# Layer 0 of a two-layer hybrid backbone: two S5 products summed by matmuls in PSUM, and the first norm's squares summed by matmuls

## The chip, the core and the metric

The kernel runs on one core of one Trainium2 chip. Its metric is the device time of one launch in microseconds; shorter is better. The engines are named as the profile names them: PE is TensorE's matmul, PEld its weight load, DVE is VectorE, ACT is ScalarE, POOL is GpSimd, SP the engine that issues the DMAs. L333 is line 333 of the kernel.

## The reference, cut to what matters

Two layers over 640 tokens (128 of a prompt and 512 of a sample) with 1024 channels. Every sub-layer starts with an RMS norm over the channels, scaled and shifted by a modulation that comes from a condition vector. Layer 0 projects the normed tokens into an S5 head group (`u`, 512 channels) and an attention head group (`q`, `k`, `v`). What matters here is the norm and how the S5 input matrix is made:

```python
def _rmsnorm(x, g):
    x32 = x.astype(jnp.float32)
    y = x32 * lax.rsqrt(jnp.mean(x32 * x32, axis=-1, keepdims=True) + EPS)
    return (y * g.astype(jnp.float32)).astype(x.dtype)
...
    lam_bar = jnp.exp(lam * jnp.exp(log_dt.astype(f32))[:, None])
    b_bar = ((lam_bar - 1) / lam)[..., None] * lax.complex(b_re.astype(f32), b_im.astype(f32))
    bu = jnp.einsum('gnp,blgp->blgn', b_bar, u.astype(jnp.complex64))
...
        hp = _modulate(_rmsnorm(xp, norm_mix_g[l]), mp[0], mp[1])
```

The kernel takes eight tokens at a time in the S5 part, so it multiplies `b_bar` by powers 0 to 8 of `lam_bar`. Real part of such a complex product: two real products and their sum.

## The kernel before, in words

Tokens lie along the free dimension and channels on the partitions, so `x` is eight tiles of 128 x 640, each worked on in two halves of 320. A long product is three matmuls of 320 columns (L205 to L207), since both factors are split into a high part (`whi`, `h00h`) and a low rest (`wlo`, `h00l`). Weights come by `weight`: a DMA into `raw`, a copy on ACT into `whi` (L194), a subtraction on POOL (or DVE) into `wlo` (L196).

The order of the instructions on each engine is not written out by hand. A scheduler sets it from priorities and from its own timeline; each engine then works its list off strictly in that order, so an instruction that waits holds up all behind it.

**The start (`start`).** ACT squares the 16 halves of `x`. The first square of each half of the tokens goes into `acc`, and each later one into `sq` and is added to `acc` by DVE (`sumsq_add`, L325). `rstd_bcast` then sums `acc` over the partitions: three matmuls for each half of the tokens, with `acc` as the stationary operand and two columns of ones as the moving one (L333), so that tokens come out on partitions. DVE makes mean plus EPS of it (L335) and an inverse square root in twelve small steps (L176 to L182), PE transposes the result into a bank (L339) and ACT copies it to `bc` (L385). The modulation runs beside this: for two blocks of columns and two halves of the channels at a time, `mod_half` multiplies the condition with weights (L282), ACT copies the row (L290), PE transposes it (L292), DVE reduces and adds it (L295, L296, L395). Then come the normalising steps, for each channel block and half (`norm_step`: L349 on DVE, L351 and L355 on ACT, L353 on DVE for even blocks, L357 on POOL for odd ones), and as each pair of blocks is done, its long products of the first three projections.

**The S5 part.** `s5_params` makes `lam_bar`, the scaled B (L716 to L722) and the powers (L744 to L749) out of some 130 small operations on DVE, at the same priority as the start. Then, for four channel blocks and two directions, `s5_unit` makes the input matrix `bp` as two products (L786, L787) and their sum (L788) on DVE, has PE transpose it in eight pieces (L793) into two banks of the tag `pb`, and has ACT copy them to `bpt` (L794), the weight of L810. L799 to L801 make the output matrix in the same manner. The units are spread over the projection of q, k, v and the attention behind it.

PSUM has eight banks: two of each of the tags `pg`, `pa`, `pb` and `pc`.

Of the kernel before, what the change touches and what calls it, by code (L numbers as in the profile page):

```python
# [11 lines left out]
F32 = mybir.dt.float32  # L12
F32R = mybir.dt.float32r
I32 = mybir.dt.int32
AF = mybir.ActivationFunctionType
ALU = mybir.AluOpType
# [5 lines left out]
HB = 320  # L22
EPS = 1e-6
NEG = -1e30
MAGIC = 12582912.0
HALVES = (slice(0, 320), slice(320, 640))
# [122 lines left out]
class Build:  # L149
# [177 lines left out]
    def rstd_bcast(self, st, tag="pc"):  # L327

        nc = self.nc
        ps = self.ps(tag)  # L330
        tiles = (0, 128, 192)
        for i, t0 in enumerate(tiles):
            nc.tensor.matmul(ps[:, 2 * i:2 * i + 2], st[0][:, t0:t0 + 128], self.ones2, start=True, stop=True)  # L333
        a = self.sp.tile([128, 3], F32, name="nrm_a", tag="nrm_a", bufs=2)
        nc.vector.tensor_scalar(a, ps[:, 0:6:2], 1.0 / 1024, EPS, op0=ALU.mult, op1=ALU.add)  # L335
        y = self.rsqrt(self.sp, a, 3, "nrm")
        bc = self.ps(tag)
        for i in (2, 1, 0):
            nc.tensor.transpose(bc[:, tiles[i]:tiles[i] + 128], y[:, i:i + 1].to_broadcast([128, 128]), self.ident)  # L339
        return bc  # L340
# [26 lines left out]
    def start(self, x, dst, P):  # L367

        nc = self.nc
        st = [self.sumsq(h) for h in range(2)]  # L370
        for k in range(8):
            for h in range(2):
                self.sumsq_add(st[h], x[k][:, HALVES[h]], nc.vector, P)
        self.mraw = "mraw", 16
        self.WX, self.WT = P, ("mraw", "mraw", 16)
        ws = [self.weight(self.A["wine"][j], 8, j) for j in range(2)]
        pairs = [[(0, 4 * n + i, kh) for n in range(2) for kh in range(2)] for i in range(4)]
        for pair in pairs:
            for m in pair:
                self.mod_load(*m, P)  # L380
        bcs = []
        for h in range(2):
            p = self.rstd_bcast(st[h], ("pg", "pa")[h])
            bc = P.tile([128, HB], F32, name="bc", bufs=2)
            nc.scalar.activation(bc, p[:, :HB], AF.Copy)  # L385
            bcs.append(bc)
        banks = [[self.ps(t) for _ in range(2)] for t in ("pg", "pa", "pb")]
        done = [0] * 3
        for i, pair in enumerate(pairs):
            md = [P.tile([128, 2, 2], F32, name=f"md{i}{n}") for n in range(2)]  # L390
            for m in pair:
                self.mod_half(*m, P, row=(P, "mrow", 2), dst=md[m[1] // 4])
            if i == 1:
                ws.append(self.weight(self.A["wine"][2], 8, 2))
            nc.vector.scalar_tensor_tensor(md[1], md[1], 1.0, self.ng[:, 0, 2 * i:2 * i + 2].unsqueeze(2).to_broadcast([128, 2, 2]),  # L395
                                           op0=ALU.add, op1=ALU.mult)
            for k in (2 * i, 2 * i + 1):
                for h in range(2):
                    self.norm_step(h, k, x[k], bcs[h], md[1][:, k % 2], md[0][:, k % 2], dst[k], True)
                for j, w in enumerate(ws):  # L400
                    for kk in range(done[j], k + 1):
                        for h in range(2):
                            self.mm_step(w, dst, h, kk, 8, banks[j][h], HB)
                    done[j] = k + 1
        w = self.weight(self.A["wine"][3], 8, 3)
        self.proj_u()
        for j in range(4):
            for h in range(2):
                if j == 3:
                    p = self.ps("pg")  # L410
                    for k in range(8):
                        self.mm_step(w, dst, h, k, 8, p, HB)
                else:
                    p = banks[j][h]
                self.ev_u(j, h, p[:, :HB])
# [354 lines left out]
    def s5_unit(self, b, d, P, U, tb):  # L770

        nc = self.nc
        V = nc.vector
        G = nc.gpsimd
        M, AD, SU = ALU.mult, ALU.add, ALU.subtract
        p0 = d * 32 + b * 8
        ps = slice(p0, p0 + 8)
        bc4 = lambda a, ax, sh: a.unsqueeze(ax).to_broadcast(sh)

        sh = [128, 8, 8, 16]  # L780
        ks = slice(0, 8) if d == 0 else slice(1, 9)
        bp = self.tl([128, 8, 128], "bp")
        t1 = self.tl([128, 8, 9, 16], "s5tmp")
        bpv = bp.rearrange("p g (s q) -> p g s q", s=8)
        B1 = self.Bb1[:, :1024].rearrange("p (a b) -> p a b", b=16)[:, ps]
        V.tensor_tensor(bpv, bc4(self.pr[:, ps, ks], 3, sh), bc4(B1, 2, sh), op=M)  # L786
        V.tensor_tensor(t1[:, :, :8], bc4(self.pi[:, ps, ks], 3, sh), bc4(self.Bb2[:, ps], 2, sh), op=M)  # L787
        V.tensor_tensor(bpv, bpv, t1[:, :, :8], op=AD)  # L788
        bpt = self.tl([128, 8, 128], "bpt")
        for r in range(2):  # L790
            pp = self.ps("pb")
            for i in range(4):
                nc.tensor.transpose(pp[:, 128 * i:128 * i + 128], bp[:, 4 * r + i], self.ident)  # L793
            nc.scalar.activation(bpt[:, 4 * r:4 * r + 4].rearrange("p a b -> p (a b)"), pp, AF.Copy)  # L794

        sh = [128, 8, 9, 16]
        ct = self.tl([128, 8, 9, 16], "ct")
        t2 = self.tl([128, 8, 9, 16], "s5tmp")
        V.tensor_tensor(ct, bc4(self.pr[:, ps], 3, sh), bc4(self.C1[:, ps], 2, sh), op=M)  # L799
        V.tensor_tensor(t2, bc4(self.pi[:, ps], 3, sh), bc4(self.C2[:, ps], 2, sh), op=M)  # L800
        V.tensor_tensor(ct, ct, t2, op=SU)  # L801

        W = self.tl([128, 8, 82], "s5g")
        e0 = 1 - d
        for r in range(2):
            pw = self.ps("pb")
            for i in range(4):
                g = 4 * r + i
                n = 128 if g < 7 else 82
                nc.tensor.matmul(pw[:, 128 * i:128 * i + n], bpt[:, g], U[:, g * 82:g * 82 + n],  # L810
                                 start=True, stop=True)
            nc.scalar.activation(W[:, 4 * r:4 * r + 4, e0:e0 + 81],
                                 pw.rearrange("p (a b) -> p a b", a=4)[:, :, :81], AF.Copy)
        ex, ez = (0, 65) if d == 0 else (64, 81)
        nc.scalar.activation(W[:, :, ex:ex + 1], self.s5x0[:, ps].unsqueeze(2), AF.Copy)
        V.memset(W[:, :, ez:ez + 1], 0.0)

        def segs(t):
            so = t[:, :, 0:65], t[:, :, 65:82]
            return so  # L820
        def tab(t):
            return (t, t[:, :, 0:17]) if d == 0 else (t[:, :, ::-1], t[:, :, 16::-1])
        sgn = self.cst[:, 400:401]
        def swap(src, name):
            o = self.tl([128, 8, 82], "s5g")
            nc.sync.dma_start(out=o[0:64], in_=src[64:128])
            nc.sync.dma_start(out=o[64:128], in_=src[0:64])
            return o
        def rotate(src, op, out):
            sw = swap(src, "sw")  # L830
            for so, c_, s_, w_ in zip(segs(src), tab(tb[:, 0]), tab(tb[:, 1]), segs(sw)):
                V.tensor_tensor(so, so, c_, op=M)
                V.scalar_tensor_tensor(w_, w_, sgn, s_, op0=M, op1=M)
            V.tensor_tensor(out, src, sw, op=op)
        Z = self.tl([128, 8, 82], "s5g")
        rotate(W, SU, Z)
        d0 = self.tl([128, 8, 82], "s5g")
        nc.scalar.activation(d0, self.s5rho[:, ps].unsqueeze(2).to_broadcast([128, 8, 82]), AF.Copy)
        V.memset(d0[:, :, ex:ex + 1], 0.0)
        V.memset(d0[:, :, ez:ez + 1], 0.0)  # L840
        Y = self.tl([128, 8, 82], "s5g")
        fl = lambda t: t.rearrange("p a b -> p (a b)")
        if d == 0:
            V.tensor_tensor_scan(fl(Y), fl(d0), fl(Z), 0.0, op0=M, op1=AD)
        else:
            V.tensor_tensor_scan(fl(Y)[:, ::-1], fl(d0)[:, ::-1], fl(Z)[:, ::-1], 0.0, op0=M, op1=AD)
        S = self.tl([128, 656], "s5s")
        Sv = S.rearrange("p (a b) -> p a b", a=8)
        rotate(Y, AD, Sv)
        fin = 81 if d == 0 else 65  # L850
        nc.scalar.activation(self.s5fin[:, p0:p0 + 8].unsqueeze(2), Sv[:, :, fin:fin + 1], AF.Copy)
        return ct, S
# [1147 lines left out]
```

## Time and profile before

| | us |
|---|---|
| median of 3 runs | 1971.04 |
| range of the runs | 1970.84 to 1973.8 |
| profiled execution, its own time | 1975.42 |
| span in its trace | 1973.2 |
| PE, PEld busy | 1798.4, 1696.1 |
| DVE, ACT, POOL busy | 1279.3, 875.5, 760.1 |

The span runs from the first to the last instruction of the profiled execution. An engine's busy time counts only its working instructions, not waits or the issue of DMAs. A busy PE is not a PE at its peak, since matmuls overlap and their ends are modelled; its clock is shown apart, as the granted share of 2.4 GHz (1.00, or 0.50 at 1.2 GHz).

### The profile page before, as it was taken

What the parts mean: (1) busy time and instruction counts of PE and PEld (TensorE: products, weight loads), DVE (VectorE), ACT (ScalarE), POOL (GpSimd) and SP (SyncE); (2) the same over time, 40 slices, a digit from 0 to 9 for tenths busy, and PEclk for the clock granted to TensorE, in tenths of its full rate; (3) what the DMA queues carried; (4) which work ended last, traced back from release to release, by engine and by line L of the source; (5) the groups of instructions that cost most, each with busy time, mean ns of one, the idle gap of its engine ahead of it and who ended that gap; (6) DMA issues with size and microseconds to landing.
All of it is one profiled execution on the core that took longest, in us unless ns stands there. A gap on an engine that the chain in (4) does not pass through costs nothing. (4 is left out here: it accounts for less than half of the span.)

```text
span 1973.2 us, 35750 instructions
## 1 busy us (share of the span) xinstructions
PE 1798.4 (91%) x13556; PEld 1696.1 (86%) x13556; DVE 1279.3 (65%) x2797; ACT 875.5 (44%) x1956; POOL 760.1 (39%) x609
## 2 busy tenths in 40 slices
PE   5789799989999999997878888798989899999998
PEld 3789677978999999997877888787878799999997
DVE  8998777269273644547589988674667927364553
ACT  4344466344243443535454455344324425344362
POOL 2522101541343343453455555522245334343451
PEclk9989899999999999998998999999999999999999
DMA  8446886533332222332576468758844122222221
GB/s 319 131 122 167 248 264 205 201 121 126 109 117 76 77 85 82 135 117 72 163 208 197 117 196 239 222 166 269 274 137 149 54 97 76 86 76 86 76 97 54
DMA packets 206983, 286.60 MB, mean 145 GB/s; under 512 B 54878, under 2 KB 138236, under 8 KB 206812
## 3 DMA queue, kind: packets, MB, share of 16 engines
q1 hardware_dynamic: 206812, 284.33, 45.4%
q8 instruction: 107, 1.75, 0.4%
q14 instruction: 64, 0.52, 0.1%
HBM read 228.87 MB, written 46.82 MB: 140 GB/s over the span
## 5 line engine op out<-in xcount | busy, mean ns | idle before, releaser
L196 POOL TENSOR_TENSOR wlo<-raw,whi 128x1024 fp32r<-128x1024 f32 (+1 forms) x153 | 359.3, 2351 | 509.1 <-ACT whi L194 462.3
L194 ACT ACTIVATE whi<-raw 128x1024 fp32r<-128x1024 f32 (+1 forms) x153 | 153.1, 1001 | 329.1 <-PE pg L206 146.8
L207 PE MATMUL pg<-hidh,wlo 128*128 128x320 f32 (+2 forms) x576 | 178.8, 311 | 0.6 <-POOL wlo L196 0.6
L205 PE MATMUL pg<-hidh,whi 128*128 128x320 f32 (+2 forms) x576 | 179.0, 311 | 0.0
L206 PE MATMUL pg<-hidl,whi 128*128 128x320 f32 (+2 forms) x576 | 178.9, 311 | 0.0
L423 DVE SCALAR_TENSOR_TENSOR x<-pg,mod,x 128x128 f32<-128x128 f32 (+2 forms) x132 | 53.7, 436 | 182.2 <-PE pg L207 182.2
L205 PE MATMUL pg<-h10h,whi 128*128 128x320 f32 x472 | 158.4, 336 | 14.7 <-DVE cb L1722 7.0
L207 PE MATMUL pg<-h10h,wlo 128*128 128x320 f32 x472 | 155.4, 329 | 1.7 <-POOL wlo L196 1.7
L206 PE MATMUL pg<-h10l,whi 128*128 128x320 f32 x472 | 155.7, 330 | 0.0
L205 PE MATMUL pa<-hidh,whi 128*128 128x320 f32 x448 | 138.0, 310 | 1.1 <-ACT whi L194 1.1
L207 PE MATMUL pa<-hidh,wlo 128*128 128x320 f32 x448 | 138.4, 309 | 0.0
L206 PE MATMUL pa<-hidl,whi 128*128 128x320 f32 x448 | 138.2, 309 | 0.0
L423 DVE SCALAR_TENSOR_TENSOR x<-pa,mod,x 128x128 f32<-128x128 f32 (+2 forms) x108 | 43.9, 435 | 133.1 <-PE pa L207 133.1
L508 POOL TENSOR_TENSOR wq<-S,wq 128x512 fp32r<-128x512 f32 x52 | 71.3, 1371 | 115.3 <-ACT wq L507 115.3
L205 PEld LDWEIGHTS pg<-h10h,whi 128*128 128x128 f32 x472 | 95.8, 203 | 18.3 <-DVE cb L1722 8.0
L207 PEld LDWEIGHTS pg<-hidh,wlo 128*128 128x128 f32 x576 | 108.2, 188 | 1.6 <-POOL wlo L196 1.1
L205 PEld LDWEIGHTS pg<-hidh,whi 128*128 128x128 f32 x576 | 108.3, 188 | 0.9 <-issue 0.8
L206 PEld LDWEIGHTS pg<-hidl,whi 128*128 128x128 f32 x576 | 108.2, 188 | 0.4 <-DVE hidl L569 0.3
L1322 DVE SCALAR_TENSOR_TENSOR cv<-cb,cw,cv 128x642 f32<-128x642 f32 x90 | 95.8, 1065 | 10.4 <-ACT cv L1319 9.2
L207 PEld LDWEIGHTS pg<-h10h,wlo 128*128 128x128 f32 x472 | 95.4, 202 | 2.1 <-POOL wlo L196 1.9
L206 PEld LDWEIGHTS pg<-h10l,whi 128*128 128x128 f32 x472 | 95.7, 203 | 0.6 <-issue 0.4
L205 PEld LDWEIGHTS pa<-hidh,whi 128*128 128x128 f32 x448 | 83.9, 188 | 2.7 <-ACT whi L194 1.8
(743 smaller groups left out, 5745.4 us busy)
## 6 DMA issues: line engine op xcount, KB each, us to landing
raw<-in_wff SPq DMA_DIRECT2D x104, 512.0 KB
mraw<-in_wmod SPq DMA_DIRECT2D x96, 512.0 KB
raw<-in_wino SPq DMA_DIRECT2D x33, 512.0 KB
rawx<-in_wff SPq DMA_DIRECT2D x24, 512.0 KB
raw<-in_wine SPq DMA_DIRECT2D x16, 512.0 KB
cka<-pd SPq DMA_DIRECT2D x28, 256.0 KB
ckb<-pd SPq DMA_DIRECT2D x28, 256.0 KB
s5g<-s5g SPq DMA_DIRECT2D x32, 164.0 KB
```

The lines of the kernel that those rows point to most:

```text
L194: nc.scalar.activation(hi[:, :kt], raw[:, :kt], AF.Copy)
L196: (nc.vector if self.lov and self.nw % self.lov else nc.gpsimd).tensor_tensor(lo[:, :kt], raw[:, :kt], hi[:, :kt], op=ALU.subtract)
L205: nc.tensor.matmul(p[:, :n], hi[:, k], xh[:, s], start=(k == 0), stop=False)
L206: nc.tensor.matmul(p[:, :n], hi[:, k], xl[:, s], start=False, stop=False)
L207: nc.tensor.matmul(p[:, :n], lo[:, k], xh[:, s], start=False, stop=(k == kt - 1))
L423: nc.vector.scalar_tensor_tensor(x[m][:, s], p[:, ls], g, x[m][:, s], op0=ALU.mult, op1=ALU.add)
L508: (V if j % 2 else nc.gpsimd).tensor_tensor(t[:, 4:8], src, t[:, 0:4], op=SU)
L1322: V.scalar_tensor_tensor(cv, cb[m][:, t:t + 642], cw[:, t:t + 1], cv, op0=M, op1=AD)
```

## The change

Two edits, both in layer 0.

In `start` the squares are no longer added up by DVE. All 16 go into `sq` (four buffers), and for each of them three matmuls add its sums over the partitions to what is in PSUM already: six banks are held for that, one for each half and token tile, with `start` at the first channel block and `stop` at the last. `rstd_bcast` reads three banks instead of one tile, and both halves use the tag `pc` for the transposes.

In `s5_unit` the sum on DVE is gone. Each of the eight pieces is made by two plain matmuls with the identity into the same place of the bank, the first with the first product as stationary operand, the second with the other.

```diff
     def rstd_bcast(self, st, tag="pc"):
...
+        if len(st) == 3:
+            for i, p in enumerate(st):
+                nc.vector.tensor_scalar(a[:, i:i + 1], p[:, 0:1], 1.0 / 1024, EPS, op0=ALU.mult, op1=ALU.add)
+        else:
+            ps = self.ps(tag)
+            for i, t0 in enumerate(tiles):
+                nc.tensor.matmul(ps[:, 2 * i:2 * i + 2], st[0][:, t0:t0 + 128], self.ones2, start=True, stop=True)
+            nc.vector.tensor_scalar(a, ps[:, 0:6:2], 1.0 / 1024, EPS, op0=ALU.mult, op1=ALU.add)
...
     def start(self, x, dst, P):
...
-        st = [self.sumsq(h) for h in range(2)]
+        tiles = (0, 128, 192)
+        sums = [[self.ps(t) for t in ("pg", "pa", "pb")] for h in range(2)]
         for k in range(8):
             for h in range(2):
-                self.sumsq_add(st[h], x[k][:, HALVES[h]], nc.vector, P)
+                sq = P.tile([128, HB], F32, name="sq", tag="sq", bufs=4)
+                nc.scalar.activation(sq, x[k][:, HALVES[h]], AF.Square)
+                for p, t0 in zip(sums[h], tiles):
+                    nc.tensor.matmul(p[:, 0:2], sq[:, t0:t0 + 128], self.ones2, start=(k == 0), stop=(k == 7))
...
-            p = self.rstd_bcast(st[h], ("pg", "pa")[h])
+            p = self.rstd_bcast(sums[h], "pc")
...
     def s5_unit(self, b, d, P, U, tb):
...
-        V.tensor_tensor(bpv, bpv, t1[:, :, :8], op=AD)
...
-                nc.tensor.transpose(pp[:, 128 * i:128 * i + 128], bp[:, 4 * r + i], self.ident)
+                o = pp[:, 128 * i:128 * i + 128]
+                nc.tensor.matmul(o, bp[:, 4 * r + i], self.ident, start=True, stop=False)
+                nc.tensor.matmul(o, t1[:, 4 * r + i, :8].rearrange("p s q -> p (s q)"), self.ident, start=False, stop=True)
```

The scheduler makes another order of it. DVE, where the norm's sums are read, before:

```order
L640 SCALAR_TENSOR_TENSOR s5t_803<-s5t_799,s5t_801 128x64
L633 TENSOR_SCALAR s5t_805<-s5t_803 128x64
L335 TENSOR_SCALAR nrm_a<-pg 128x3
L640 SCALAR_TENSOR_TENSOR s5t_807<-s5t_805,s5t_803 128x64
L176 TENSOR_SCALAR nrm_t<-nrm_a 128x3
```

and after (`s5t` are the small tiles of `s5_params`; L636 and L642 of the changed kernel are L627 and L633 of the one before, L334 reads a sum):

```order
L636 TENSOR_TENSOR s5t_949<-s5t_929,s5prm 128x64
L636 TENSOR_TENSOR s5t_951<-s5t_939,s5prm 128x64
L636 TENSOR_TENSOR s5t_953<-s5t_949,s5t_951 128x64
L334 TENSOR_SCALAR nrm_a<-pg 128x1
L636 TENSOR_TENSOR s5t_955<-s5t_953,s5t_937 128x64
L642 TENSOR_SCALAR s5t_957<-s5t_955,cst 128x64
L334 TENSOR_SCALAR nrm_a<-pa 128x1
```

Ahead of the first of these reads stood 24 operations of `s5_params`; now 84 stand there, up to its division and the scale of B.

DVE at the last pair of channel blocks of the norm, before (L349 normalises, `pw` and `pwr` are the powers):

```order
L353 SCALAR_TENSOR_TENSOR h00l_125<-nf,md_569,h00h_124 128x192
L353 SCALAR_TENSOR_TENSOR h00l_125<-nf,md_569,h00h_124 128x320
L349 SCALAR_TENSOR_TENSOR nf<-x_103,md_570,bc 128x320
L719 TENSOR_TENSOR Bb_924<-s5bc_753,s5t_911 128x1024
L744 TENSOR_TENSOR pw<-pwr 128x32
L745 TENSOR_TENSOR pw<-pwi 128x32
L746 TENSOR_TENSOR pwr<-pw 128x32
```

and after (L353 of the changed kernel is L349 of the one before, L730 and L731 are L721 and L722, L753 to L758 are L744 to L749):

```order
L295 TENSOR_REDUCE mtmp<-pc 128x4
L730 TENSOR_TENSOR Bb_960<-Bb_960,Btmp 128x1024
L755 TENSOR_TENSOR pwr<-pw 128x32
L296 TENSOR_TENSOR md_606<-mtmp,bmod 128x4
L731 TENSOR_SCALAR Bb_960<-Bb_960,cst 128x1024
L756 TENSOR_TENSOR pw<-pwr,pwi 128x32
L757 TENSOR_TENSOR pw<-pwi,pwr 128x32
L404 SCALAR_TENSOR_TENSOR md_606<-md_606,ng 128x4
L758 TENSOR_TENSOR pwi<-pw 128x32
L353 SCALAR_TENSOR_TENSOR nf<-x_102,md_606,bc 128x128
```

The scaled B and the powers of the first direction, which all stood behind the norm's last step, now stand ahead of the last pair of blocks.

PE at the first S5 unit, before (`h00h` and `h00l` are the normed tokens, 311 long products stand ahead of L793):

```order
L207 MATMUL pg<-h00h_124,wlo 128x320
L205 MATMUL pg<-h00h_126,whi 128x320
L206 MATMUL pg<-h00l_127,whi 128x320
L793 MATMUL pb<-cst,bp 128x128 x8
L207 MATMUL pg<-h00h_126,wlo 128x320
```

and after, with 221 long products ahead of it:

```order
L206 MATMUL pg<-h00l_115,whi 128x320
L802 MATMUL pb<-cst,bp 128x128 x2
L207 MATMUL pg<-h00h_114,wlo 128x320
L205 MATMUL pg<-h00h_116,whi 128x320
L206 MATMUL pg<-h00l_117,whi 128x320
L207 MATMUL pg<-h00h_116,wlo 128x320
L205 MATMUL pg<-h00h_118,whi 128x320
L803 MATMUL pb<-cst,s5tmp 128x128
L802 MATMUL pb<-cst,bp 128x128
L803 MATMUL pb<-cst,s5tmp 128x128
```

The eight transposes have become two kinds of matmul, L802 and L803, that alternate, and the unit stands 90 long products earlier in PE's list.

ACT at the squares, after (L194 copies weights; before, all 16 squares stood ahead of both copies):

```order
L379 ACTIVATE sq<-x_99 128x320 x2
L379 ACTIVATE sq<-x_100 128x320
L194 ACTIVATE whi<-raw 128x1024
L379 ACTIVATE sq<-x_100 128x320
L194 ACTIVATE whi<-raw 128x1024
L379 ACTIVATE sq<-x_101 128x320 x2
L379 ACTIVATE sq<-x_102 128x320 x2
L379 ACTIVATE sq<-x_103 128x320 x2
```

Six of the squares now stand behind the second copy.

## Rows read from the trace of the kernel before

**Rows 1.** The page: busy us, share, instructions; busy tenths in 40 slices.

```profile
PE 1798.4 (91%) x13556; PEld 1696.1 (86%) x13556; DVE 1279.3 (65%) x2797; ACT 875.5 (44%) x1956; POOL 760.1 (39%) x609
...
DVE  8998777269273644547589988674667927364553
```

**Rows 2.** Windows, us: length, busy PE, PEld, DVE, ACT, POOL, clock, DMA, GB/s.

```profile
31.00:64.60 33.60, 29.36 (x223) 22.05 (x216) 33.36 (x103) 18.08 (x44) 17.66 (x16) 1.00 0.46 174
81.50:201.20 119.70, 107.58 (x790) 105.16 (x788) 108.16 (x156) 45.69 (x91) 34.15 (x19) 0.94 0.54 149
201.20:260.00 58.80, 46.55 (x389) 37.31 (x388) 47.14 (x95) 29.64 (x84) 3.55 (x4) 0.91 0.86 257
99.70:104.00 4.30, 4.28 (x19) 4.28 (x20) 4.30 (x9) 1.79 (x4) 0.00 (x0) 0.55 0.01 2
135.00:140.00 5.00, 4.86 (x21) 4.86 (x22) 5.00 (x14) 1.98 (x6) 0.00 (x0) 0.50 0.30 88
```

**Rows 3.** Timeline of the start: start us, us, engine line op, [idle before <-releaser].

```profile
6.45 0.83 ACT L320 ACTIVATE acc<-x 128x320 f32<-128x320 f32 x2 [2.54 <-DMA x<-in_xT]
6.55 0.48 DVE L640 SCALAR_TENSOR_TENSOR s5t<-s5t,s5t 128x64 f32<-128x64 f32 x2
...
12.88 0.35 DVE L627 TENSOR_TENSOR s5t<-s5prm,s5t 128x64 f32<-128x64 f32 x2
13.15 0.89 DVE L325 TENSOR_TENSOR acc<-acc,sq 128x320 f32<-128x320 f32 x2
...
15.70 4.68 POOL L196 TENSOR_TENSOR wlo<-raw,whi 128x1024 fp32r<-128x1024 f32 x2 [14.44 <-ACT whi L194]
15.81 1.06 ACT L194 ACTIVATE whi<-raw 128x1024 fp32r<-128x1024 f32 x1 [0.19 <-DMA raw<-in_wine]
15.82 4.64 DVE L640 SCALAR_TENSOR_TENSOR s5t<-s5t,s5t 128x64 f32<-128x64 f32 x2
...
16.40 1.42 PE L333 MATMUL pa<-cst,acc 128*128 128x2 f32 x6
...
17.75 1.93 PE L282 MATMUL pc<-mraw,scond 128*32 128x256 f32 x16
...
20.61 0.15 DVE L335 TENSOR_SCALAR nrm_a<-pg 128x3 f32<-128x3 f32 x1
...
24.02 0.90 PE L339 MATMUL pg<-cst,nrm_y 128*128 128x128 f32 x3 [4.34 <-DVE nrm_y L182]
...
30.25 1.73 DVE L349 SCALAR_TENSOR_TENSOR nf<-x,md,bc 128x128 f32<-128x128 f32 x5
...
57.15 0.54 DVE L349 SCALAR_TENSOR_TENSOR nf<-x,md,bc 128x320 f32<-128x320 f32 x1
...
64.59 0.41 ACT L1055 ACTIVATE us<-pg 128x128 f32<-128x128 f32 x1 [5.21 <-PE pg L207]
...
86.21 1.23 DVE L786 TENSOR_TENSOR bp<-pwr,Bb 128x1024 f32<-128x1024 f32 x1
```

**Rows 4.** Timeline of PE at a later norm, full clock.

```profile
403.08 0.72 PE L333 MATMUL pc<-cst,acc 128*128 128x2 f32 x6
403.66 0.39 PE L206 MATMUL pa<-ct,whi 128*128 128x320 f32 x1
```

**Rows 5.** Line 788: duration in ns (min, median, max), first and last start.

```profile
L788 DVE TENSOR_TENSOR bp<-bp,s5tmp x8: 1214/1218/1227, 98.5 to 238.5; 128x1024 f32<-128x1024 f32 x8
```

**Rows 6.** Timeline of PE at the S5 units.

```profile
99.72 1.97 PE L793 MATMUL pb<-cst,bp 128*128 128x128 f32 x8 [5.42 <-DVE bp L788]
105.50 1.91 PE L810 MATMUL pb<-s5s,bpt 128*128 128x128 f32 x16
...
135.14 1.11 PE L793 MATMUL pb<-cst,bp 128*128 128x128 f32 x4 [4.35 <-DVE kk L910]
...
241.85 1.04 PE L793 MATMUL pb<-cst,bp 128*128 128x128 f32 x8
```

**Rows 7.** Waits of PE, 60 to 260 us: total, times, longest.

```profile
PE pc L1105 <- ACT qs L1090: 6.2, 2, 5.1
```

More of the change, by code (lines that the diff above doesn't have):

```diff
@@ L329, in rstd_bcast @@
         nc = self.nc
-        ps = self.ps(tag)
         tiles = (0, 128, 192)
-        for i, t0 in enumerate(tiles):
-            nc.tensor.matmul(ps[:, 2 * i:2 * i + 2], st[0][:, t0:t0 + 128], self.ones2, start=True, stop=True)
         a = self.sp.tile([128, 3], F32, name="nrm_a", tag="nrm_a", bufs=2)
-        nc.vector.tensor_scalar(a, ps[:, 0:6:2], 1.0 / 1024, EPS, op0=ALU.mult, op1=ALU.add)
+        if len(st) == 3:
[6 more added lines that the diff above has]
+            nc.vector.tensor_scalar(a, ps[:, 0:6:2], 1.0 / 1024, EPS, op0=ALU.mult, op1=ALU.add)
         y = self.rsqrt(self.sp, a, 3, "nrm")
@@ L386, in start @@
             bcs.append(bc)
+        del sums, p
         banks = [[self.ps(t) for _ in range(2)] for t in ("pg", "pa", "pb")]
```

## The prediction

> **What bounds the kernel now.** I read the page first: its busy times and its slices, for the engine that is busy nearly everywhere. TensorE (PE) is at 91% of the span, VectorE (DVE) at 65%, but the first three slices of DVE (some 150 us) read 8, 9, 9 [rows 1]. So the kernel is PE's, except at its head, where both edits lie. Next I cut that head into stretches, by where PE's long products stand. From 31.0 to 64.6 us DVE is busy 33.4 of 33.6 us and PE 29.4; from 81.5 (240 long products done, of the layer's 768) to 201.2 (all 768 done) PE is busy 107.6 of 119.7 at a granted clock of 0.94; from 201.2 to 260.0, the attention, 46.6 of 58.8 at 0.91 [rows 2]. So PE stands still for 12.1 us in the middle stretch and 12.2 us in the last. Its clock takes 119.7 x 0.06 = 7.2 us and 58.8 x 0.09 = 5.3 us more. After 260 us PE is nearly full, and what its queue has lost by then it keeps: I count every microsecond at the head as one at the end. Last I looked at what ends PE's idle time. The two long waits of the middle stretch, 5.42 and 4.35 us, stand right before the S5 transposes of line 793, and DVE ended both [rows 6].
>
> **The S5 matrices.** DVE loses the addition of line 788, eight times, 1.22 us each, 9.8 us [rows 5]. PE pays. Eight transposes ran in 1.04 us at full clock, so one costs (1.04 - 0.27) / 7 = 0.11 us, the 0.27 being the tail of the last. A plain f32 product of the same size is two records: line 810 had 16 of them in 1.91 us, (1.91 - 0.27) / 15 = 0.109 each, 0.22 for a product [rows 6]. A unit had 8 transposes (0.9 us) and gets 16 products (3.5 us), 2.6 us more; eight units, **+21.0 us** of PE time at full clock. At half the clock a transpose took (1.97 - 0.42) / 7 = 0.22 us [rows 6], so a unit would cost 5.2 us more there; I take the full clock, as only two of the eight groups started slow.
>
> What hides these 21 us is idle time of PE behind DVE. If DVE is early enough at line 793, the two waits go (9.8 us), and so does most of the slow clock behind them: 4.3 us at 0.55 from 99.7 and 5.0 us at 0.50 from 135 [rows 2] are 1.9 + 2.5 = 4.4 us. Of the 17.5 us that the attention loses, the longest wait, 5.1 us on ACT behind the last projection [rows 7], can be filled, since products of the sixth and seventh unit now stand there; I take 4 us. So **R = 18 us** come back. At the least one DVE wait goes with its clock, 9 us; at the most all of 19.3 and some 14 of 17.5, 33 us.
>
> **The norm's squares.** DVE loses 14 additions at a pace of 0.45 us, 6.2 us; PE gains 96 records in place of 12. ACT squares as before, 0.42 us each from 6.45 on. At the clock that PE shows there, six records take 1.35 us (16.40 to 17.75) [rows 3]: 96 x 0.225 = 21.6 us, from 6.9 to 28.5 us. At full clock six took 0.58 (403.08 to 403.66) [rows 4]: 9.3 us in all, and then ACT's order decides, where six squares now stand behind the second weight copy (15.81 + 1.06): 16.9 + 6 x 0.42 + 0.6 = 20 us. Which clock it is, no row shows; both ends are kept.
>
> It matters less than it seems, because DVE's order moved too. The first sum is read behind 84 S5 operations, where it stood behind 24. An S5 operation takes 0.18 to 0.24 us (pairs of 0.35 and 0.48), so 60 more are 10.5 to 14.1 us, less the 6.2 of the additions: the read at 20.61 goes to 24.9 to 28.5 [rows 3]; I take 27 us, **6.4 later**. Behind it 51 operations stand before both inverse roots are there; 33 took 3.4 us between the read and the transposes at 24.02, 0.10 each, so these take 5.4 us: 32.4. From the transposes to the first normalising step it was 6.2 us. The modulation products that ran ahead of the sums (16 in 1.93) now lie in that way, and the lag of the second root is gone from it; I take 6 us. So the first normalising step comes at 38 us instead of 30.25, **+8**, with 6 and 10 as ends.
>
> From there to the last normalising step it was 26.9 us [rows 3], DVE full [rows 2]. Of what lies between, 46 small S5 operations are gone (8 to 11 us), but 27 small ones on the powers and four large ones on the scaled B (lines 719 to 749) stand ahead of the last pair's steps: 27 x 0.18 to 0.24 and four of line 788's size, 4.9 us [rows 5], make 10 to 11 us. That is +1. And POOL's long operations come into this stretch: two S5 operations, 0.48 us as a pair at 6.55, took 4.64 us at 15.82 beside two of POOL that took 4.68 [rows 3], so each POOL operation cost DVE 2.1 us; three more of them are 6.3. PE, which waited for weights at the end of the stretch, now has them early; for that I take 3 us back. Together +4, with -5 and +11 as ends. So the third projection ends at about 77 us instead of 64.6: **D = +12 us**, from 1 to 21. On DVE itself the lighter load shows behind that: its line 786, at 86.2 before [rows 3], should come at about 80, and with PE 12 us late that is why PE's waits should go.
>
> **Sum.** D + 21.0 - R = 12 + 21 - 18 = **+15 us**; the ends are 1 + 21 - 33 = -11 and 21 + 21 - 9 = +33. The profiled run took 1975.4 us (span 1973.2), 4.4 above the median of 1971.0; on it the sum makes 1990.4, on the median **1986.0**.
>
> **Rivals.** (a) *DVE was what PE followed all along.* If the norm's chain is not late (D = 1, its additions gone) and DVE, 16 us lighter, lets PE run through all the waits (R = 31), the time is 1971 + 1 + 21 - 31 = 1962, faster. For it: DVE at 33.4 of 33.6 us. Against: PE itself is busy for 107.6 of 119.7, and its order lets the last normalising steps come behind 60 S5 operations. It wins where R passes 21 us plus D. (b) *The head is not late, but PE then meets DVE again*: D = 2, R = 17, 1977. In PE's order only 221 long products stand ahead of the first S5 group, 311 before, so an early PE waits there. (c) *Nothing comes back*: PE comes to the S5 groups just as early as its operands, and the waits only change their place: D = 12, R = 4, 2000.
>
> What the last one would do at its worst, the whole price of 21 us on top of D with no idle time filled, is 2004. The Trainium skill says the same without a condition (Perfetto Trace Analysis, section Transposes: a logical transpose should be a transpose and not a standard matmul). The two waits of 5.42 and 4.35 us speak against taking it unconditionally, since in them a product costs nothing.
>
> **How the numbers follow.** My forecast, +15, has 0.60; (a) 0.16; (b) 0.15; (c) 0.09. What this kernel's measurement can tell from no change is about 0.2%, 4 us. The forecast's own spread (D and R) lies nearly all above +4; (b) is above it at its middle and within it for a third; (a) is faster for nearly all of it. With some of the forecast's lower end, that makes faster 0.17, the same 0.08, slower 0.75. The range runs from 1967, which takes in (b) and the nearer part of (a), to 2002, which takes in (c); some 0.18 is left outside, mostly (a).
>
> **What would show it.** In the changed profile: (1) the first normalising step at about 38 us and the last at 65 to 77; if the last is at 57 as before, D is wrong. (2) A group of 16 products in about 3.5 us, two records each. (3) No wait of PE on DVE at the S5 groups; if waits of 3 us or more stand there, (b) or (c). (4) The records of the sums at 1.35 us for six up to 28 us, or 0.58 and done at 20. (5) All 768 long products done at 210 to 220 us instead of 201. The order of PE changes far beyond layer 0's head, and what that shifts later I count as nothing; several microseconds of either sign there would make the sum wrong without any of these steps.

## The result, and the profile after

The changed kernel took 1994.6 us (median of 4 runs, 1992.56 to 1998.26), the kernel before, on the same chip, 1972.42: 22 us more, ratio 1.0104 with a 95% interval of 1.0081 to 1.0127. Measured again on another occasion it took 1995.66 against 1974.32, ratio 1.0116 (1.0093 to 1.0138). The profiled execution took 1993.4 us, its span is 1991.6. The forecast was 1986.0, +15 us, in a range of 1967 to 2002.

The page after, answering to [rows 1] (busy us, share, instructions; busy tenths in 40 slices):

```profile
PE 1835.5 (92%) x13832; PEld 1735.1 (87%) x13832; DVE 1277.2 (64%) x2779; ACT 872.5 (44%) x1956; POOL 759.2 (38%) x609
...
DVE  7985586448545463728689997865656936364553
```

PE is busy 37.1 us longer, DVE 2.1 us less. The rest of this document measures with three landmarks that every kernel has: the first read of the third projection's bank (the end of the head), the last of the layer's 768 long products (the end of the projections), and the **gate**, the first product on PE that takes `L` (in both kernels right after a wait of 1.50 us on ACT). Windows between these landmarks, after (length, busy PE, PEld, DVE, ACT, POOL, clock, DMA share, GB/s):

```profile
0.00:79.62 79.62, 59.00 (x379) 48.39 (x380) 67.40 (x239) 30.89 (x68) 25.97 (x28) 0.96 0.56 211
79.62:223.29 143.67, 134.37 (x1018) 131.91 (x1017) 100.84 (x153) 54.87 (x112) 42.17 (x24) 0.98 0.55 155
223.29:377.19 153.90, 143.86 (x1232) 114.85 (x1230) 112.47 (x245) 86.52 (x252) 13.56 (x14) 0.99 0.71 220
```

and before, cut at its own landmarks:

```profile
0.00:64.59 64.59, 40.34 (x295) 28.16 (x296) 56.99 (x218) 30.77 (x68) 23.06 (x26) 1.00 0.68 260
64.59:200.94 136.35, 123.38 (x896) 120.92 (x895) 124.56 (x184) 53.56 (x108) 43.82 (x26) 0.95 0.55 152
200.94:354.24 153.30, 136.84 (x1163) 109.03 (x1161) 114.68 (x252) 88.46 (x256) 14.84 (x14) 0.97 0.74 231
```

Read the lengths first: the head is 15.0 us longer, the projections 7.3, the attention 0.6, together 22.95. Then the busy PE: +18.7, +11.0 and +7.0. What PE did not pay for by standing still is the difference: its idle time fell by 3.6, 3.7 and 6.4 us.

The start after, answering to [rows 3] (start us, us, engine line op, [idle before <-releaser]; L381 are the sums, L334 reads one, L343 transposes the roots, L353 is a normalising step, L357 and L361 its low part, L196 a weight's low part, L729 the scaled B):

```profile
7.20 0.56 PE L381 MATMUL pa<-cst,sq 128*128 128x2 f32 x2
...
26.71 0.15 DVE L334 TENSOR_SCALAR nrm_a<-pg 128x1 f32<-128x1 f32 x1
26.83 0.57 PE L381 MATMUL pb<-cst,sq 128*128 128x2 f32 x2
...
32.23 1.56 PE L343 MATMUL pc<-cst,nrm_y 128*128 128x128 f32 x6 [4.83 <-DVE nrm_y L182]
33.17 0.44 ACT L393 ACTIVATE bc<-pc 128x320 f32<-128x320 f32 x1 [10.33 <-PE pc L343]
33.72 3.38 PE L282 MATMUL pc<-mraw,scond 128*32 128x256 f32 x32
...
38.76 2.60 DVE L353 SCALAR_TENSOR_TENSOR nf<-x,md,bc 128x128 f32<-128x128 f32 x5
...
47.49 5.20 POOL L196 TENSOR_TENSOR wlo<-raw,whi 128x1024 fp32r<-128x1024 f32 x2 [2.30 <-ACT whi L194]
48.17 2.18 DVE L296 TENSOR_TENSOR md<-mtmp,bmod 128x4 f32<-128x4 f32 x1
...
69.40 1.22 DVE L729 TENSOR_TENSOR Btmp<-s5bc,s5t 128x1024 f32<-128x1024 f32 x1
...
73.36 1.73 DVE L353 SCALAR_TENSOR_TENSOR nf<-x,md,bc 128x128 f32<-128x128 f32 x5
74.58 0.63 PE L205 MATMUL pg<-h00h,whi 128*128 128x320 f32 x1 [7.03 <-ACT h00h L355]
```

The sums keep PE busy from 6.75 to 27.4 us. Then PE stands still for 4.83 us until the roots are there, although 32 modulation products (L282) were next; these start at 33.72, right behind ACT's copy of the root (33.17 + 0.44), which empties a bank of `pc`. The first normalising step is at 38.76. PE waits 7.03 us for the last pair.

An S5 unit on PE after, answering to [rows 6], where a group of eight transposes was 0.9 us at full clock:

```profile
131.23 0.39 PE L802 MATMUL pb<-cst,bp 128*128 128x128 f32 x2
131.46 0.39 PE L803 MATMUL pb<-cst,s5tmp 128*128 128x128 f32 x2
...
134.58 0.39 PE L803 MATMUL pb<-cst,s5tmp 128*128 128x128 f32 x2
134.72 0.39 PE L205 MATMUL pg<-h00h,whi 128*128 128x320 f32 x1
```

Sixteen products in 134.72 - 131.23 = 3.49 us. PE's waits after, from 79 to 223 us (total, times, longest):

```profile
PE pb L915 <- DVE ct L811: 4.6, 1, 4.6
PE pc L1103 <- ACT qs L1100: 2.8, 2, 1.4
PE pb L803 <- DVE s5tmp L796: 1.4, 1, 1.4
```

The two waits of [rows 6] are gone, but 4.6 us stand one step on, where PE takes the S5 output matrix `ct` from DVE. And DVE now waits for PE, which it did nowhere from 80 to 210 us in the kernel before:

```profile
DVE bp L795 <- PE pb L802: 16.0, 3, 12.8
```

`bp` has one buffer, so DVE can't write the next unit's `bp` before PE has read this one's. PE's list spreads some units among long products (one of them from 190.22 to 206.5 us, which is the wait of 12.8). All kernels here with the S5 edit have such a wait, 10 us or more, and none of the others has one above 2.2 us.

### The profile page after: what moved, and what is told of

Read it like the earlier page. It is cut to its first block, busy times and chain, and to the rows that moved or that the text cites. A ratio compares the mean times of both kernels' runs of the same rounds, so it can differ in the third digit from the quotient of the medians.

```text
span 1991.6 us, 36304 instructions
## 1 busy us (share of the span) xinstructions
PE 1835.5 (92%) x13832; PEld 1735.1 (87%) x13832; DVE 1277.2 (64%) x2779; ACT 872.5 (44%) x1956; POOL 759.2 (38%) x609
## 4 chain that ended last, share of the span: by engine, by line
PE 27%; DVE 12%; DMA 7%; issue 2%; POOL 1%; ACT 1%; SPq 1%; POOLq 0%; DVEq 0%; ACTq 0%
PE pg L205 4%; PE pg L206 4%; PE pg L207 3%; DVE cv L1332 2%; DVE sbt L1435 2%; PE pa L207 2%; PE pa L206 2%; PE pa L205 2%; DVE ub L1437 1%; DMA cgq<-gbd 1%; PE pg L535 1%; PE pg L537 1%; PE pg L536 1%; PE pb L535 1%; PE pa L535 1%
## 5 line engine op out<-in xcount | busy, mean ns | idle before, releaser
L196 POOL TENSOR_TENSOR wlo<-raw,whi 128x1024 fp32r<-128x1024 f32 (+1 forms) x153 | 355.4, 2326 | 512.3 <-ACT whi L194 461.7
L194 ACT ACTIVATE whi<-raw 128x1024 fp32r<-128x1024 f32 (+1 forms) x153 | 152.9, 1000 | 319.3 <-PE pg L206 131.4
L205 PEld LDWEIGHTS pg<-h10h,whi 128*128 128x128 f32 x472 | 96.1, 204 | 15.6 <-ACT cb L1324 8.3
```

Of the source, the lines that this page charges most:

```text
L194: nc.scalar.activation(hi[:, :kt], raw[:, :kt], AF.Copy)
L196: (nc.vector if self.lov and self.nw % self.lov else nc.gpsimd).tensor_tensor(lo[:, :kt], raw[:, :kt], hi[:, :kt], op=ALU.subtract)
L205: nc.tensor.matmul(p[:, :n], hi[:, k], xh[:, s], start=(k == 0), stop=False)
```

## The experiments

Theory: both edits cost, one at the head (norm) and one as PE time (S5), and idle time of PE gives back a part. Rivals: only the head loses; only the products lose; DVE is what PE follows.

All kernels in one table (us; landmarks of the profiled execution; the median is set against the kernel before on the same chip in the same stretch of runs, with the ratio's 95% interval).

| kernel | head ends | projections end | gate | median, against before | ratio |
|---|---|---|---|---|---|
| before | 64.6 | 200.9 | 354.2 | | |
| changed | 79.6 | 223.3 | 377.2 | +22.2 | 1.0081 to 1.0127 |
| e1_norm | 79.9 | 211.7 | 359.6 | +2.2 | 0.9994 to 1.0028 |
| e2_s5 | 66.7 | 219.1 | 370.2 | +19.2 | 1.0065 to 1.0126 |
| e3_nosum | 64.4 | 203.2 | 352.2 | +0.4 | 0.9991 to 1.0030 |
| e3b_late | 80.3 | 214.2 | 361.6 | -2.9 | 0.9966 to 0.9999 |
| e14_plain | 64.2 | 214.2 | 364.9 | +0.6 | 0.9998 to 1.0027 |
| e8_bank | 75.1 | 220.8 | 369.2 | +4.8 | 1.0010 to 1.0039 |
| e9_f32r | 65.3 | 218.7 | 371.8 | +10.3 | 1.0036 to 1.0073 |
| e10_f32r_norm | 65.4 | 201.5 | 357.3 | -4.7 | 0.9967 to 1.0000 |

**The norm's edit alone** (e1_norm). The S5 hunk undone:

```diff
+        V.tensor_tensor(bpv, bpv, t1[:, :, :8], op=AD)
...
-                nc.tensor.matmul(o, bp[:, 4 * r + i], self.ident, start=True, stop=False)
-                nc.tensor.matmul(o, t1[:, 4 * r + i, :8].rearrange("p s q -> p (s q)"), self.ident, start=False, stop=True)
+                nc.tensor.transpose(pp[:, 128 * i:128 * i + 128], bp[:, 4 * r + i], self.ident)
```

> The kernel before with the norm's edit alone (squares summed by matmuls in PSUM); the S5 sums stay on DVE. Theory (both edits cost, and PE's waits give back a part): the third projection ends near 79.6 us as with both edits (+15 on the kernel before), and PE, that much later at the S5 transposes, no longer waits there for DVE (5.42 and 4.35 us go, with most of the slow clock behind them, 4.4 us), so the time is +0 to +6 us. Rival (the head alone makes the loss): no wait comes back, the time is +15 to +22 us, and the S5 products cost nothing. Rival (the products alone make the loss): within 2 us of the kernel before and the third projection near 65 us.

The head ends 15.3 us late, as with both edits. By the gate 9.9 of it have come back:

```profile
359.63 0.41 PE L205 MATMUL pg<-L,whi 128*128 128x320 f32 x1
```

Where the kernel before waits 1.50 us for ACT at this line, here there is no wait. But the two waits on DVE did not both go, as the theory had it. The one on `bp` is gone; the other, on `kk`, stands in two places (79 to 212 us; L802 are the transposes here):

```profile
PE pb L947 <- DVE kk L919: 4.2, 1, 4.2
PE pb L802 <- DVE kk L919: 3.5, 1, 3.5
```

Of the 9.9 us, PE's idle time gave 3.3 in the projections and 4.4 in the attention, and its busy time fell by 2.2. The time is within what can be told from no change. The rival that the head makes the whole loss falls.

**The S5 edit alone** (e2_s5). The hunks of `start` and `rstd_bcast` undone, the S5 hunk kept.

> The kernel before with the S5 edit alone (two products summed in one bank); the norm as before. Theory: PE gets 21 us of extra products, the head stays where it was (third projection at 64.6 us), DVE is 1.2 us lighter for each unit, and about half of the price falls into waits: +8 to +14 us. Rival (the head alone makes the loss): the products lie in idle time, -4 to +3 us. Rival (the products alone make the loss): +17 to +22 us.

The head is where it was (2.1 us late), and the gate comes 16.0 us late:

```profile
370.24 0.41 PE L205 MATMUL pg<-L,whi 128*128 128x320 f32 x1 [1.49 <-ACT L L1185]
```

The theory's 8 to 14 us was too low; at the gate it lies between the theory and the rival that the products alone make the loss, and the median (+19) is that rival's. At the end the two edits add up: 2.2 + 19.2 = 21.4 us, against 22.2 for both.

**DVE's additions taken away with nothing in their place** (e3_nosum, norm as before):

```diff
-        V.tensor_tensor(bpv, bpv, t1[:, :, :8], op=AD)
```

> The kernel before with the addition of the two S5 products left out on DVE and nothing put in its place: the transposes take the first product alone, so part of the S5 input matrix is missing. It shows what DVE's 9.8 us are worth by themselves. Theory: the two waits before the S5 transposes shrink by the additions ahead of them (1.2 us and some 5 us), -4 to -8 us; with the S5 edit alone standing 15 to 21 us above it, which is what the extra products cost net. Rival (DVE is what PE follows all along): -10 us or more. Rival (DVE is no bound there): within 2 us.

DVE is freed of 9.8 us and the gate moves by 2.0, no more than between two executions of the kernel before (2.1, see the last experiment). PE's two waits at the transposes were 5.4 us on `bp` and 4.4 on `kk` [rows 6]; without the additions (64 to 203 us) they are:

```profile
PE pb L792 <- DVE kk L909: 5.6, 1, 5.6
PE pb L792 <- DVE bp L786: 3.6, 1, 3.6
```

Together 9.2 instead of 9.8. The longer one is not for `bp` at all: `kk` is a small step of DVE that reads a bank of `pb`, so there the transposes waited for a bank, and the additions are not in it. DVE's own waits show where the freed time went (80 to 210 us; before, then without the additions):

```profile
DVE s5g L832 <- DMA s5g<-s5g: 10.0, 3, 5.9
DVE s5g L832 <- DMA rt<-rt: 2.2, 2, 1.7
```

```profile
DVE s5g L831 <- DMA s5g<-s5g: 10.9, 3, 6.6
DVE s5g L831 <- DMA rt<-rt: 8.7, 2, 8.5
```

DVE waits 7.4 us longer for the S5 chain's DMAs. What it saves it spends waiting, so "DVE is no bound there" is what the runs support, and the theory's -4 to -8 us is wrong. The S5 edit alone stands 18.0 us above this kernel at the gate: that is what the products cost there.

**The same with the norm's edit** (e3b_late): the changed kernel with `nc.tensor.transpose` of `bp` in place of the two products.

> The changed kernel without the second product: one transpose of the first S5 product for each piece and no sum anywhere, so part of the S5 input matrix is missing. The norm's edit stays. Against the changed kernel it shows what the 21 us of extra products cost while the head is late; with the norm's edit alone it differs by DVE's additions. Theory (the products cost nearly their whole price, DVE's additions little): the gate of layer 0 is reached 17 to 21 us before the changed kernel (at 356 to 360 us), within 4 us of the norm's edit alone; the time is 15 to 22 us below the changed kernel. Rival (products and late head fill the same waits, so a price without the head's delay would not show): 10 us or less below the changed kernel.

The gate is at 361.6, 15.6 us before the changed kernel (the theory said 17 to 21) and 2.0 behind the norm's edit alone. So with the head late a little more of the price is hidden than without, 5.4 of 21 us instead of 3.0, and DVE's additions are again worth nothing. Against before the median is 2.9 us lower, though the gate is 7.3 us late, so the time lies 25 us below the changed kernel's and not 15 to 22; more on that below.

**The price alone** (e14_plain): transposes of the kernel before as plain products, DVE's work unchanged.

```diff
-                nc.tensor.transpose(pp[:, 128 * i:128 * i + 128], bp[:, 4 * r + i], self.ident)
+                nc.tensor.matmul(pp[:, 128 * i:128 * i + 128], bp[:, 4 * r + i], self.ident, start=True, stop=True)
```

> The kernel before with its 64 transposes of the S5 input matrices issued as plain products with the identity; the sum stays on DVE. Nothing but PE's price is changed: 64 x (0.218 - 0.109) = 7.0 us at full clock. Theory (a product costs its price nearly everywhere, the two DVE waits stay in front of the groups): the gate of layer 0 at 358 to 362 us (354.2 before), the time +4 to +8 us. Rival (idle time of PE takes it up): gate within 1.5 us of before, time within 2 us.

Busy PE between head and gate is 7.7 us more (130.56 + 137.38 against 123.38 + 136.84), about the 7.0 that were worked out. The gate is 10.6 us late, more than the price, as the scheduler made another order and new waits, among them 3.8 us on a weight copy in the projections:

```profile
PE pg L205 <- ACT whi L194: 3.8, 1, 3.8
```

Yet the time is +0.6 us, nothing that can be told from no change. Neither side of the expectation holds whole: the gate says price and more, the end says nothing.

**What holds the modulation back** (e8_bank): the changed kernel with the roots in banks that the sums have left.

```diff
-            p = self.rstd_bcast(sums[h], "pc")
+            p = self.rstd_bcast(sums[h], ("pg", "pa")[h])
```

(with the references to the read sums dropped first, so that the banks are free).

> The changed kernel, but the transposes of the inverse roots go into banks of pg and pa, which the sums have left by then, and not into the two banks of pc. In the changed kernel the modulation products needed a bank of pc and started at 33.72 us, right behind the copies that emptied them, though PE had stood idle from 27.4 to 32.2. Theory (the banks hold the modulation behind the roots): the products run ahead of the roots, the first normalising step comes at 34 to 36 us instead of 38.8, the time is 2 to 5 us below the changed kernel. Rival (the sums at half the clock and DVE's order alone set the head): the products move, the first normalising step stays within 1 us of 38.8 and the time within 2 us.

PE at the start, and DVE's first and last normalising steps (L355 here):

```profile
19.74 1.08 PE L282 MATMUL pc<-mraw,scond 128*32 128x256 f32 x8
...
29.61 2.77 PE L282 MATMUL pc<-mraw,scond 128*32 128x256 f32 x20
...
32.94 0.87 PE L345 MATMUL pg<-cst,nrm_y 128*128 128x128 f32 x3
```

```profile
34.82 1.74 DVE L355 SCALAR_TENSOR_TENSOR nf<-x,md,bc 128x128 f32<-128x128 f32 x5
...
67.47 1.73 DVE L355 SCALAR_TENSOR_TENSOR nf<-x,md,bc 128x128 f32<-128x128 f32 x5
73.43 0.55 DVE L355 SCALAR_TENSOR_TENSOR nf<-x,md,bc 128x320 f32<-128x320 f32 x1
```

The banks did hold the modulation: its products now run ahead of the roots, and the first step comes 3.9 us earlier. The last pair gains less, since on DVE the S5 powers still stand ahead of it (51.57 to 67.47). The gate is 8.0 us earlier than in the changed kernel, and the time 17 us lower, where 2 to 5 was expected: again more at the end than at the gate.

**What makes the head late** (e9_f32r: both edits, and e10_f32r_norm: the norm's edit alone). Banks as in e8_bank, and squares and ones as fp32r, which makes a sum one record:

```diff
-                sq = P.tile([128, HB], F32, name="sq", tag="sq", bufs=4)
+                sq = P.tile([128, HB], F32R, name="sq", tag="sq", bufs=4)
```

> The changed kernel with the roots' transposes in the banks of pg and pa, and the squares and the ones kept as fp32r, so that a sum is one record and not two. Theory (the sums' own time at half the clock and the order that follows from it set the head): the sums end at 17 to 20 us instead of 27.2, the first normalising step comes at 28 to 32 us, the third projection at 66 to 70 us, gate 366 to 371 us with the dear S5 products in it; 4 to 8 us below the kernel that has the banks alone. Rival (DVE's own work sets the head): sums early, but the last normalising step stays at 70 us or later and the time within 3 us of the banks alone.

> The norm's edit alone (the S5 sums stay on DVE), with the roots' transposes in the banks of pg and pa and squares and ones as fp32r. Theory: with the head no later than before and 6 us of additions off DVE, gate 350 to 354 us and the time 0 to 5 us below the kernel before. Rival (DVE meets PE again at the S5 transposes): the early head is lost there, gate 354 to 358 us, time 0 to 4 us above the kernel before.

PE's last sum in e9_f32r, and DVE's normalising steps:

```profile
16.97 0.35 PE L385 MATMUL pb<-ones2r,sq 128*128 128x2 f32 x1
17.37 1.08 PE L282 MATMUL pc<-mraw,scond 128*32 128x256 f32 x8
```

```profile
29.13 1.72 DVE L355 SCALAR_TENSOR_TENSOR nf<-x,md,bc 128x128 f32<-128x128 f32 x5
...
51.45 2.59 DVE L355 SCALAR_TENSOR_TENSOR nf<-x,md,bc 128x320 f32<-128x320 f32 x1
```

The sums end at 17.3 instead of 27.4, the first step is 9.6 us earlier, the last 25, and the head ends at 65.3, 0.7 behind the kernel before. So nearly the whole 15 us of the head hang on the banks (4.5 us, e8_bank), on the sums' records (9.8 us more) and on the order that follows from them, and the rival that DVE's own work sets the head falls. But the gate gains only 5.4 us of these 14.3 (371.8, where 366 to 371 was expected), and e9_f32r's time is not 4 to 8 us below that of the kernel with the banks alone. Each set against before, it is +10.3 against +4.8, the other way. PE, early again, meets DVE again (e10_f32r_norm, 64 to 202 us):

```profile
PE pb L807 <- DVE kk L924: 6.0, 1, 6.0
PE pb L807 <- DVE bp L802: 3.9, 1, 3.9
```

That is the rival of e10_f32r_norm at the gate (357.3), while its time came out below before, and level with it in more rounds (n4_f32r_norm, next).

**The same kernels once more** (n1_before: before; n2_after: changed; n3_bank: e8_bank; n4_f32r_norm: e10_f32r_norm), for how much executions of one order differ.

> The kernel before, once more, with a profile: how much two executions of one kernel differ stage by stage. Theory (the order of instructions sets the head, and what differs between executions lies behind layer 0): the third projection within 0.5 us of 64.6 and the gate within 2 us of 354.2, the stretch from there to the end anywhere within 6 us of 1619. Rival (the head too differs from execution to execution): gate off by 4 us or more, and the differences read at the gate are worth no more than that.

> The changed kernel once more, in more rounds. Theory: 18 to 23 us above the kernel before (ratio 1.009 to 1.012), the gate within 2 us of 377.2. Rival (the 23 us at the gate are not kept to the end): a ratio of 1.006 or less.

> The changed kernel with the roots' transposes in the banks of pg and pa, once more: its gate was 15 us behind the kernel before, its end level with it. Theory (the scheduler's later order is another one, and better by some 10 us): the stretch from the gate to the end is again 1600 to 1610 us, and it is shorter in the stretch between 880 and 1510 us. Rival (that was one execution's luck): 1613 us or more.

> The norm's edit alone with roots' transposes in the banks of pg and pa and the squares as fp32r, in more rounds. Theory (it gains by its later order, not at the head, where its gate is 3 us late): 1 to 5 us below the kernel before, ratio 0.9975 to 0.9995. Rival (no difference): 0.9995 to 1.0010.

The gates came at 356.3, 379.8, 370.5 and 358.9, up to 2.6 us from the first time. From the gate to the end it took 1618.1 (1619.0 the first time), 1605.4 (1614.4), 1607.4 (1603.3) and 1618.4 us (1610.5). n4_f32r_norm was 1.8 us below before, ratio 0.9978 to 1.0019: no difference, which was the rival. So the stretch up to the gate repeats within 2 to 3 us, and one order varies by up to 9 us behind it. e8_bank was under 1610 us there both times, before over 1618 both times, as the theory on its later order said; but the changed kernel was once under 1610 too, so two executions each are thin, and the medians (10 us better than the gate for e8_bank, none for the changed kernel) carry more. Most of these differences lie in layer 1's mixer, from the first long product that takes `h10h` to the first that takes `h13h`. Its window in the changed kernel, first and second time:

```profile
903.14:1528.47 625.33, 541.39 (x4654) 505.34 (x4650) 474.92 (x1078) 288.75 (x651) 289.73 (x313) 0.93 0.62 190
```

```profile
903.38:1521.82 618.44, 534.64 (x4653) 500.05 (x4649) 472.95 (x1078) 288.87 (x651) 289.18 (x313) 0.93 0.63 192
```

Before it took 627.30 and 626.24 us there, e8_bank 613.68 and 619.38.

## Why the prediction was right, and where it was not

**The head, +12: measured +15.0.** The chain came as worked out: first sum read at 26.71 (27), roots on PE at 32.23 (32.4), first normalising step at 38.76 (38). The mis-sized term is the stretch from the first to the last step: +10.8 us (38.76 to 76.48, against 26.9 before), where 1 + 6.3 = 7.3 was taken. Behind the last step 4.3 us came back (3.1 us to the end of the head, against 7.4), where 3 was taken. So 8.5 + 10.8 - 4.3 = 15.0. The parts of the stretch were named: the powers and the scaled B stand ahead of the last pair, most of the time from 59 to 73 us, and POOL's long operations blocked small ones (an addition of 128 x 4 took 2.18 us at 48.17). Of such blocks the forecast counted three more than before, 6.3 us. In the trace there are five in this stretch (at 48.17, 50.71, 53.58, 56.44 and 63.20 us, together 10.0 us longer than their like) against one before (2.2 us), so 7.8 us more; the remaining 2 us were not taken apart. The Trainium skill has it as a rule (SBUF — State Buffer, section SBUF: two separate sides: when a DVE operation with two SBUF inputs and a GpSimd operation that reads SBUF want the shared port, the loser blocks for the whole instruction); the row agrees. And e9_f32r, where the powers lie behind the last pair, has it at 51.45. One reason was incomplete: that the modulation's products lay behind the roots was read from the order. That the two banks of `pc` held them there, e8_bank had to show.

**The price, +21.0: right.** 3.5 us for a group was forecast, 3.49 measured. How much of it remains at the gate depends on the kernel around it: 18.0 in e2_s5 against e3_nosum, 15.6 in the changed kernel against e3b_late, 14.5 in e9_f32r against e10_f32r_norm.

**What comes back, R = 18: measured 13.1** (15.0 + 21.0 - 22.95). The failed step is "the two waits go (9.8 us)". They went, and others came: PE's idle time in the projections fell by 3.7 only. The clock gave 3.0 where 4.4 was taken (worked out: busy PE behind the head rose by 18.0 instead of 21; granted clock 0.95 to 0.98 and 0.97 to 0.99), the attention 6.4 instead of 4. 3.7 + 3.0 + 6.4 = 13.1. The step also gave a wrong reason: a lighter DVE. One of the two waits was for a bank, not for the addition, and e3_nosum shows that DVE's additions were worth at most 2 us at the gate. What shortens PE's idle time is PE being late: e1_norm, with the additions still on DVE, got 9.9 us back. The lower end of R, 9 us, was added up too high as well: the longer wait with its clock is 5.42 + 1.9 = 7.3.

**"Every microsecond at the head is one at the end": not shown.** For the changed kernel it looks so: gate +23 in both comparisons, median +22.2 and +21.3. But e3b_late, e14_plain and e8_bank end some 10 us better than their gates say (-2.9 for +7.3, +0.6 for +10.6, +4.8 for +15.0), e9_f32r 7 us better, and e2_s5 3 us worse (+19.2 for +16.0). The prediction counted such shifts as nothing and named them as what could make the sum wrong. The two misses, 3 us at the head and 5 in what comes back, made the forecast 8 us too low at the gate. That it is also about 7 too low at the end, and not right on the spot or 10 us further off, is luck: it rests on a later order that neither gained nor lost, and nothing in the prediction could foresee that. Why those orders end better is open: the windows place it mostly in layer 1's mixer for e8_bank, and no run took that stage apart.

**The projections' end, 210 to 220 us: 223.3**, out of the range for the same reasons.

**The rivals.** (a) is refuted by e3_nosum: a lighter DVE alone does not let PE run on. (b) is what happens when the head is not late: in e9_f32r and e10_f32r_norm the waits on DVE return. (c) at R = 4 was too dark, but its mechanism, waits that only change their place, took 6.1 of the 9.8 us. The rule cited with it, that a logical transpose should be a transpose and not a standard matmul (the Trainium skill, Perfetto Trace Analysis, section Transposes), agrees with busy PE in e14_plain, +7.7 us, and does not show in that kernel's time.

## What to carry to other kernels

Work moved to the busiest engine costs its price wherever that engine isn't already waiting, and work taken from another engine gains only if that engine doesn't wait itself: look at its waits too, not at its busy share. An edit that holds more PSUM banks can stop unrelated work that needs one; the sign is an engine that idles with ready work next and starts just as a bank is emptied. Where a scheduler makes the order, split the trace at landmarks, and compare a stage only after seeing how much one kernel's own executions differ there.

## What was not expected of the hardware

The sums are 96 records in a row, where the norm before had two lots of six, and over 20 us they never ran faster than 0.213 us a record (three products, six records, in 1.28 us), while at 403 us six took 0.58 [rows 4]. The prediction put that down to the clock. The granted clock of the stretch reads 1.00 all the same:

```profile
7.00:27.00 20.00, 20.00 (x95) 20.00 (x96) 18.32 (x78) 8.31 (x17) 4.70 (x2) 1.00 1.01 396
```

The sums are not alone in it. The 32 modulation products that took 3.38 us at 33.72, in a stretch that reads 1.00 too, took little more than half of that 4 us later:

```profile
37.98 1.93 PE L282 MATMUL pc<-mraw,scond 128*32 128x256 f32 x32
```

In the kernel before, a transpose of the root lasted 0.42 us at 24 us and 0.27 from 409 us on. So all of PE's work at the start ran at about half its later pace, up to some 37.5 us here and 28.7 before, though PE was busy without a gap from 6.75 to 27.4 us. In such a stretch the reading of the clock can't be relied on; the pace of a known product can. What ended the slow stretch isn't shown. An fp32r record took the same 0.213 us (e9_f32r: 16.97 less the one before at 16.76); the gain there is one record in place of two.
